# Operand blocks of the down product summed by accumulating transfers instead of VectorE, and the last pair's steps in another order

## The chip, the core and the metric

One core of a Trainium2 chip runs the whole program. The metric is the device time of one execution in microseconds. The kernel before takes 1924.49 us, the median of 3 runs (1922.67 to 1926.2).

## The reference, cut to what matters

The kernel computes one layer of a decoder for 1024 prompt tokens with 16 meta tokens ahead of them and 8 samples. Two of its parts are feed-forward blocks of the same form, one at the start and one at the end; the change touches only these.

```python
D_MODEL, D_FF = 1024, 2816

def swiglu(x, wg, wu, wd):
    return (jax.nn.silu(x @ wg) * (x @ wu)) @ wd

h = h + 0.5 * swiglu(rmsnorm(h, n1), w1g, w1u, w1d)     # first FFN, 1048 token columns here
...                                                     # HGRN2 and Mamba-2 groups, output projection
h = h + 0.5 * swiglu(rmsnorm(h, n2), w2g, w2u, w2d)     # second FFN, 1032 token columns here
```

All arithmetic is float32 in effect: each operand of a matmul is split into a high and a low part, and three matmuls (high by high, high by low, low by high) make one product.

## The kernel before, in words

**How a feed-forward block is tiled.** `ffn` takes the 22 column tiles of gate and up as 11 pairs of tiles (a and b), and then `down`. Each 2 by 2 block product is done with seven block products instead of eight, which needs sums of blocks as operands. The products of a pair are numbered 1 to 7. In `chained_pair` the string `STEPS[kind]` gives their order for the four kinds of pair, `plain`, `first`, `both` (all the middle ones) and `last`. A name such as `a5` is product 5 of tile a and makes two steps (one for each half c of the tokens), each of 12 matmuls of 262 or 258 columns; `N15` or `M4` is one step with products of the same scheme applied a second time, inside product 2 (N) or 3 (M); it has 6 matmuls for each digit. A pair of kind `both` or `first` has 28 steps.

**What sets the order.** The order is written out by hand. `Steps.run` emits, before step i, everything that was placed at i, then the matmuls of the step, then its evacuation. The tables `PLAIN`, `FIRST`, `BOTH`, `LAST` and `DOWN` place each small piece of work at a step counted from the pair's (or down's) first step; a number past the pair's end falls into the next pair. In the names of the pairs' tables, d loads a weight block, s sums two of them, h and l make the high part (ScalarE) and the low part (VectorE), g multiplies the gate by the norm and applies silu, p multiplies gate by up into the hidden tile, S and D are the stores and sums below, R is the restore below. TensorE, VectorE, ScalarE and SyncE then do their instructions in the order in which they were emitted; the order on GpSimd's queue is left to the scheduler.

**PSUM banks.** In the pairs there are two double banks for accumulation. Products 1, 6, 7 and 4 of a tile share one, 5 and 3 another. A new one can begin only when one of the two has been read for the last time.

**The hidden blocks.** A pair leaves four blocks of 128 x 524 (or 516): a0, a1, b0, b1, in two tiles of the tag "s" (8 slots, six of which hold operands of the inner products during the middle pairs). `down` reads them as the right operands of its seven products, from seven DRAM tensors in `Hidden.d`: operand 1 is a0, 2 is b0, 3 is b1, 7 is b1+a1, 5 is a1+a0, 6 is b1+a1+a0 and 4 is b0+b1+a1+a0. Before the change VectorE makes the four sums in place (`Hidden.sum_`, L1070), and SyncE stores each operand (L1073) between them. `down` (L1107) then loads each operand in six groups (L1090), and ScalarE and VectorE split them (L1094, L1098).

**Keep and restore.** The inner products M overwrite the first half of one operand of product 3. GpSimd's queue copies it to DRAM beforehand (`keep`, L580), and in the last pair, which computes product 3 again in the plain way, copies it back (`restore`, L585).

The functions that the diff touches follow, with the lines of the profile.

## Time and profile before

The profiled execution took 1926.8 us by the clock of the runs, and its span in the profile is 1925.1 us.

| | |
|---|---|
| median of 3 runs | 1924.49 us |
| profiled execution / its span | 1926.8 / 1925.1 us |
| TensorE (PE) busy | 1896.4 us, 99% |
| VectorE (DVE) busy | 1561.9 us, 81% |
| ScalarE (ACT) busy | 942.1 us, 49% |
| GpSimd (POOL) busy | 87.3 us, 5% |
| bytes moved | 260.61 MB, mean 135 GB/s |
| first FFN: pairs / down | to about 472 us / 472 to about 698 us |
| second FFN: pairs / down | about 1205 to 1681 us / 1681 us to the end |

How to read it: matmuls are pipelined, so a busy TensorE is not one at its peak. The number of matmuls in a stretch of fixed length tells more: a stretch of 5 us at full pace shows 43 or 44 of them (those that reach over an edge are counted in both stretches). "PEclk" is the share of its full clock that TensorE was granted. "A <- B" in a view of waits reads: A stood idle until B ended.

### The profile page before, as it was taken

How to read it: one execution, taken by the hardware profiler on the slowest of the kernel's cores; microseconds unless marked ns; L12 is line 12 of the kernel's file. 1: busy time of each engine (PE TensorE's matmuls, PEld its weight loads, DVE VectorE, ACT ScalarE, POOL GpSimd, SP SyncE). 2: the span in 40 equal slices, each digit the busy share in tenths (PEclk: the TensorE clock that was granted, in tenths of full speed). 3: DMA queues.
4: the chain of work that ended last, by engine and by line, in shares of the span. 5: the costliest groups of instructions: out<-in, count | busy, mean ns of one | idle time of the engine just before them, and what ended most of it. 6: DMA issues, size and time to landing. Idle time of an engine off the chain costs nothing.

```text
span 1925.1 us, 41201 instructions
## 1 busy us (share of the span) xinstructions
PE 1896.4 (99%) x16480; PEld 1861.2 (97%) x16480; DVE 1561.9 (81%) x2953; ACT 942.1 (49%) x1856; POOL 87.3 (5%) x167
## 2 busy tenths in 40 slices
PE   9999999999999999999999999999999999999998
PEld 8999999998999999999999989999999999899997
DVE  7899999998688877576776667989999999868965
ACT  7644444444533644466554465743444444453353
POOL 3000000000000410000000002200000000000000
PEclk9999999999999999999999999999999999999999
DMA  8242323346977551132444254323234233597862
GB/s 240 67 125 84 111 84 112 92 120 180 279 219 258 162 164 51 50 101 71 133 139 113 58 167 149 101 84 98 83 99 116 83 116 100 166 278 219 281 183 79
DMA packets 325801, 260.61 MB, mean 135 GB/s; under 512 B 17953, under 2 KB 299809, under 8 KB 325601
## 3 DMA queue, kind: packets, MB, share of 16 engines
q1 hardware_dynamic: 324213, 255.80, 44.2%
q8 instruction: 129, 2.11, 0.5%
q0 software_dynamic: 1376, 2.17, 0.4%
q14 instruction: 63, 0.52, 0.1%
q10 hardware_dynamic: 20, 0.01, 0.0%
HBM read 192.91 MB, written 65.08 MB: 134 GB/s over the span
## 4 chain that ended last, share of the span: by engine, by line
PE 86%; DVE 7%; DMA 3%; ACT 2%; issue 1%; SPq 0%; DVEq 0%; POOL 0%; ACTq 0%; POOLq 0%
PE acc L163 24%; PE acc L165 23%; PE acc L164 23%; PE mis L165 3%; PE mis L163 3%; PE mis L164 3%; DMA hd<-s 1%; DMA u<-hd 1%; DVE t L806 1%; PE mis L2108 1%; DVE u L1098 1%; DVE ws L470 1%; DVE r L462 1%; ACT u L348 1%; PE mis L1734 0%
## 5 line engine op out<-in xcount | busy, mean ns | idle before, releaser
L163 PE MATMUL acc<-u,ws 128*128 128x258 f32 (+4 forms) x3922 | 1150.3, 294 | 4.8 <-DVE t L806 1.9
L165 PE MATMUL acc<-u,ws 128*128 128x258 f32 (+4 forms) x3922 | 1137.6, 290 | 5.4 <-DVE ws L470 5.3
L164 PE MATMUL acc<-u,ws 128*128 128x258 f32 (+4 forms) x3922 | 1136.7, 290 | 1.9 <-DVE u L1098 1.6
L163 PEld LDWEIGHTS acc<-u,ws 128*128 128x128 f32 x3922 | 741.4, 189 | 13.0 <-issue 3.4
L164 PEld LDWEIGHTS acc<-u,ws 128*128 128x128 f32 x3922 | 744.1, 190 | 4.3 <-DVE u L1098 2.1
L165 PEld LDWEIGHTS acc<-u,ws 128*128 128x128 f32 x3922 | 740.4, 189 | 6.9 <-DVE ws L470 6.5
L466 ACT CAST ws<-r 128x512 fp32r<-128x512 f32 x232 | 143.1, 622 | 246.2 <-DVE r L462 107.0
L470 DVE TENSOR_TENSOR ws<-r,ws 128x512 fp32r<-128x512 f32 x232 | 157.7, 689 | 12.9 <-ACT ws L466 12.7
L462 DVE TENSOR_TENSOR r<-r,r 128x512 f32<-128x512 f32 x168 | 116.0, 692 | 6.2 <-DMA r<-in_w_ffn_up_dram 5.3
L1098 DVE TENSOR_TENSOR u<-u,u 128x1048 fp32r<-128x1048 f32 (+3 forms) x84 | 96.8, 1159 | 20.2 <-ACT u L1094 20.2
L819 ACT COPY t<-acc 128x524 f32<-128x524 f32 (+1 forms) x116 | 68.4, 590 | 84.8 <-PE acc L165 83.7
L873 ACT ACTIVATE t<-t 128x524 f32<-128x524 f32 (+1 forms) x80 | 51.2, 639 | 94.8 <-DVE t L806 94.6
L1094 ACT CAST u<-u 128x1048 fp32r<-128x1048 f32 (+3 forms) x84 | 82.8, 988 | 21.5 <-DMA u<-hd 21.4
L158 DVE TENSOR_TENSOR ws<-r,ws 128x512 fp32r<-128x512 f32 x88 | 61.0, 704 | 35.0 <-ACT ws L157 33.9
L165 PE MATMUL mis<-u,ws 128*128 128x258 f32 (+1 forms) x310 | 87.9, 284 | 0.5 <-DVE ws L615 0.5
L1162 ACT CAST ws<-u 128x512 fp32r<-128x512 f32 (+1 forms) x72 | 42.1, 585 | 94.7 <-DVE u L1157 91.4
L163 PE MATMUL mis<-u,ws 128*128 128x258 f32 (+1 forms) x310 | 88.0, 284 | 0.0
L164 PE MATMUL mis<-u,ws 128*128 128x258 f32 (+1 forms) x310 | 87.8, 283 | 0.0
L806 DVE TENSOR_TENSOR t<-t,u 128x524 f32<-128x524 f32 (+1 forms) x120 | 83.6, 697 | 2.0
L1191 DVE SCALAR_TENSOR_TENSOR s<-acc,s 128x524 f32<-128x524 f32 (+3 forms) x86 | 53.9, 650 | 32.0 <-PE acc L165 31.7
L1162 ACT CAST ws<-r 128x512 fp32r<-128x512 f32 (+1 forms) x84 | 48.1, 581 | 62.2 <-DVE r L1157 31.9
L1167 DVE TENSOR_TENSOR ws<-r,ws 128x512 fp32r<-128x512 f32 (+1 forms) x84 | 57.0, 694 | 19.1 <-ACT ws L1162 19.0
(486 smaller groups left out, 2734.4 us busy)
## 6 DMA issues: line engine op xcount, KB each, us to landing
r<-in_w_ffn_down_dram SPq DMA_DIRECT2D x128, 256.0 KB
hd<-s SPq DMA_DIRECT2D x93, 258.0 KB
r<-in_w_ffn_gate_dram SPq DMA_DIRECT2D x88, 256.0 KB
r<-in_w_ffn_up_dram SPq DMA_DIRECT2D x88, 256.0 KB
hd<-s SPq DMA_DIRECT2D x77, 262.0 KB
u<-hd SPq DMA_DIRECT2D x36, 516.0 KB
u<-hd SPq DMA_DIRECT2D x28, 524.0 KB
r<-in_w_in_dram SPq DMA_DIRECT2D x56, 256.0 KB
```

The costliest lines, as they stand in the source:

```text
L158: self.nc.vector.tensor_sub(lo, src, hi.bitcast(F32))
L163: mm(ps, whi, xhi, start=first, stop=False, skip_group_check=more)
L164: mm(ps, whi, xlo, start=False, stop=False, skip_group_check=more)
L165: mm(ps, wlo, xhi, start=False, stop=last, skip_group_check=more)
L462: self.K.nc.vector.tensor_tensor(self.raw[p], self.raw[x], self.raw[y], op)
L466: self.K.nc.scalar.copy(self.w[p][:, : self.n * P], self.raw[p])
L470: self.K.nc.vector.tensor_sub(t[:, 512 : 512 + w], self.raw[p], t[:, :w].bitcast(F32))
L806: nc.vector.tensor_mul(t, t if src is None else src, spread.lanes(int(n[1]), slice(0, 2)))
L819: nc.scalar.copy(temp(x, {1: "z", 6: "v", 7: "w"}[p]), ps)
L1094: K.nc.scalar.copy(hi, lo.bitcast(F32))
L1098: K.nc.vector.tensor_sub(lo, lo.bitcast(F32), hi.bitcast(F32))
L1162: nc.scalar.copy(w[p, j, g][:, : n * P], src)
```

## The change

1. The four sums leave VectorE. `Hidden.put` stores a first block into each of the seven DRAM tensors from SyncE (S1, S2, S3, S4, S5, S6, S7), and then adds the other blocks to those tensors with transfers of GpSimd's queue that accumulate in DRAM (A5, A6, A7, A4, then B6, B4, then C4). A transfer that adds to a tensor waits for the one before on the same tensor. There are 88 fewer instructions on VectorE, 154 more transfers on GpSimd's queue, and 154 stores as before.
2. In the last pair product 3 of each tile comes ahead of product 4: "a5 M4 a3 a4 b1 N15" for "a5 M4 a4 b1 a3 b6 N15", and "N4 b3 b4" at the end for "b4 N4 b3".
3. The restored half is written over another operand of M (product 5's, in a slot of the tag "s"), which is free earlier: the restore stands at step 4 and no longer at step 13. The second half (c = 1) of product 3 of tile b, and of tile a, reads its first two blocks from there.
4. All five tables place their pieces anew.

```diff
-def product(K, ps, w, op, n, first, last, more=False):
+def product(K, ps, w, op, n, first, last, more=False, k0=0):
...
     def restore(self):
-        for x, d in self.kept:
+        for x, (_, d) in zip(self.op[5], self.kept):
             self.K.nc.gpsimd.dma_start(x, d)
...
-    "last": "a1 M15 a6 M62 a7 M73 a5 M4 a4 b1 a3 b6 N15 b7 N62 b5 N73 b4 N4 b3",
+    "last": "a1 M15 a6 M62 a7 M73 a5 M4 a3 a4 b1 N15 b6 N62 b7 N73 b5 N4 b3 b4",
...
 FIRST = {
...
-    33: "ga0 Mh3 Ml2", 34: "pa0", 35: "Ml3 S1", 37: "ga1 S2", 40: "gb1", 43: "pb1", 45: "S3 pa1", 47: "D7", 49: "S7", 50: "D6 D5", 51: "D4 S5",
-    52: "S4", 55: "S6",
+    30: "S2", 31: "Mh2", 33: "ga0 Ml2", 34: "Mh3 pa0 Ml3", 37: "ga1 S1", 40: "gb1", 43: "pb1", 45: "pa1", 46: "S5", 47: "S3 S7 S6", 49: "A7 A6 A4",
+    51: "A5", 52: "B6 B4", 55: "C4",
 BOTH = {
...
-    48: "D5", 49: "S7", 50: "D6 S5", 53: "D4 S4", 59: "S6",
+    46: "A5 A7 A6", 47: "S3", 49: "B4", 50: "B6 C4",
 LAST = {
...
-    15: "Nh3 N- Nl1", 17: "hb5 Nl3", 18: "Nh2", 19: "ga1 Nl2", 20: "hb4 lb5", 22: "pa1", 23: "lb4", 26: "hb3", 27: "ga0", 28: "pa0", 30: "lb3 S1",
-    31: "gb0 pb0", 32: "gb1", 34: "S2 pb1", 36: "S3 D7", 37: "D5 S7", 39: "S5", 40: "D6", 42: "S6 D4 S4",
+    14: "N- Nh3", 15: "lb6 ga1 Nl1", 18: "Nh2 pa1 Nl2", 19: "Nl3", 20: "hb5", 22: "lb5", 24: "hb3 hb4", 25: "ga0 lb3", 27: "lb4 pa0", 28: "S5",
+    29: "gb0 S1", 31: "gb1", 32: "pb0 S2", 33: "pb1", 34: "S4", 36: "S3 S7 S6", 38: "A5 A4 A7", 39: "A6 B4", 41: "B6", 45: "C4",
...
-        product(K, ps[:, c], lefts[x].w[p], ops[c].op[p], 4, p == b, True, p != b)
+        if (kind, p, c) == ("last", 3, 1):
+            for (hi, lo), k0 in ((inners["M"].op[5], 0), ([t[:, 2 * K.Q :] for t in ops[c].op[p]], 2)):
+                w = lefts[x].w[p]
+                product(K, ps[:, c], w, (hi, lo), 2, False, k0 == 2, True, k0)
+        else:
+            product(K, ps[:, c], lefts[x].w[p], ops[c].op[p], 4, p == b, True, p != b)
...
-    def sum_(self, hid, p):
-        t, x = (self.block(hid, n) for n in {7: (3, 12), 5: (12, 1), 6: (7, 1), 4: (2, 6)}[p])
-        self.K.nc.vector.tensor_add(t, t, x)
-    def store(self, i, hid, p):
-        self.K.nc.sync.dma_start(self.d[p][:, :, i, :], halves(self.block(hid, p)))
+    def put(self, i, hid, name):
+        p, n = int(name[1]), {"S1": 0, "S5": 1, "S2": 2, "S4": 2, "S3": 3, "S7": 3, "S6": 3, "A5": 0, "A7": 1, "A6": 1, "A4": 3, "B6": 0, "B4": 1, "C4": 0}[name]
+        t = halves(hid[n // 2][0][:, n % 2 * 2 * self.K.Q : n % 2 * 2 * self.K.Q + 2 * self.K.Q])
+        if name[0] == "S":
+            self.K.nc.sync.dma_start(self.d[p][:, :, i, :], t)
+        else:
+            self.K.nc.gpsimd.dma_start(self.d[p][:, :, i, :], t, accum_op=ALU.add)
```

Three places show how the instructions move. The first is VectorE's queue in the last pair of the first FFN where tile a gives way to tile b. The line numbers shift by two to five: L824 and L834 of before are L829 and L839, L877 is L879. A row of L806 with an "acc" as source reads product 4 from its bank for the last time; L824 and L834 (now L829 and L839) do so for products 3 and 5; L462 sums two weight blocks, L470 makes a low part. Before:

```order
L834 TENSOR_TENSOR t_5448<-acc_5477,t_5448 128x524
L806 TENSOR_TENSOR t_5448<-t_5448,u_846 128x524
L470 TENSOR_TENSOR ws_5491<-r_5395,ws_5491 128x512
L637 TENSOR_TENSOR t_5257<-mis_5343,t_5257 128x262
L806 TENSOR_TENSOR t_5257<-t_5257,u_846 128x524
L462 TENSOR_TENSOR r_5264<-r_5475,r_5264 128x512
L806 TENSOR_TENSOR t_5548<-acc_5310,u_846 128x524
L877 TENSOR_TENSOR s_5413<-t_5013,t_4958 128x524
L877 TENSOR_TENSOR s_5308<-t_5257,t_5198 128x524
```

After:

```order
L462 TENSOR_TENSOR r_5293<-r_5505,r_5293 128x512
L470 TENSOR_TENSOR ws_5539<-r_5339,ws_5539 128x512
L462 TENSOR_TENSOR r_5554<-r_5425,r_5293 128x512
L829 TENSOR_TENSOR t_5419<-acc_5507,t_5419 128x524
L879 TENSOR_TENSOR s_5336<-t_5287,t_5228 128x524
L879 TENSOR_TENSOR s_5443<-t_5038,t_4981 128x524
L601 TENSOR_TENSOR r_5273<-r_5273,r_5425 128x256
L602 TENSOR_TENSOR r_5273<-r_5273,u_1545 128x256
L470 TENSOR_TENSOR ws_5551<-r_5293,ws_5551 128x512
L806 TENSOR_TENSOR t_5419<-t_5419,u_846 128x524
L615 TENSOR_TENSOR ws_5568<-u_1545,ws_5568 128x512
L806 TENSOR_TENSOR t_5621<-acc_5341,u_846 128x524
```

Before, products 5 and 3 of tile a hold their bank (acc_5477) until a3, which stands behind b1, so b1 takes the bank that product 4 leaves (L806 from acc_5310). Now a3 has left its bank (L829, acc_5507) eight rows ahead of product 4's row (L806 from acc_5341), and b1 takes that one; the whole of a4 stands between a3 and b1.

The second is VectorE's queue at the end of the same pair. Before, ws_5778 is the low part for product 3 of tile b, the pair's last product; now ws_5775 is that low part and ws_5777 is the one for product 4, which is the pair's last. L637 is a piece of an inner product, L1098 (now L1095) and L1167 (L1164) split operands and weights of `down`. Before:

```order
L834 TENSOR_TENSOR t_5714<-acc_5741,t_5714 128x524
L806 TENSOR_TENSOR t_5714<-t_5714,u_846 128x524
L637 TENSOR_TENSOR t_5337<-mis_5674,t_5337 128x262
L637 TENSOR_TENSOR t_5337<-u_1544,t_5337 128x262
L637 TENSOR_TENSOR t_5589<-u_1544,t_5589 128x262
L806 TENSOR_TENSOR t_5337<-t_5337,u_846 128x524
L1098 TENSOR_TENSOR u_5641<-u_5641,u_5640 128x1048
L877 TENSOR_TENSOR s_5697<-t_5337,t_5548 128x524
L806 TENSOR_TENSOR t_5827<-acc_5559,u_846 128x524
L1167 TENSOR_TENSOR ws_5762<-r_5661,ws_5762 128x512
L637 TENSOR_TENSOR t_5589<-mis_5666,t_5589 128x262
L470 TENSOR_TENSOR ws_5778<-r_5554,ws_5778 128x512
```

After:

```order
L806 TENSOR_TENSOR t_5369<-t_5369,u_846 128x524
L470 TENSOR_TENSOR ws_5775<-r_5554,ws_5775 128x512
L839 TENSOR_TENSOR t_5773<-acc_5805,t_5773 128x524
L806 TENSOR_TENSOR t_5773<-t_5773,u_846 128x524
L470 TENSOR_TENSOR ws_5777<-r_5483,ws_5777 128x512
L879 TENSOR_TENSOR s_5659<-t_5369,t_5621 128x524
L1095 TENSOR_TENSOR u_5703<-u_5703,u_5702 128x1048
L637 TENSOR_TENSOR t_5652<-mis_5668,t_5652 128x262
L1164 TENSOR_TENSOR ws_5803<-r_5591,ws_5803 128x512
```

The low part stood eleven instructions behind product 5's evacuation (L834) and now stands ahead of it (L839); the low part for the product that comes last now stands two behind it.

The third is GpSimd's queue from the keeping on. The names hd_109, hd_111, hd_112 and hd_114 are the operands 6, 5, 7 and 4. Before, the two copies out and the two back are followed at once by work of the groups behind the FFN:

```order
L580 DMA kp_1214<-u_546 128x524
L580 DMA kp_1215<-u_548 128x524
L585 DMA u_548<-kp_1215 128x524
L585 DMA u_546<-kp_1214 128x524
L232 TENSOR_TENSOR t_7573<-t_7573,t_7577 128x262
L232 TENSOR_TENSOR t_7575<-t_7575,t_7580 128x262
```

After, the part that belongs to the pair of kind `first`, with what each transfer waits for (DMASW is an earlier transfer of this queue, DMAHW one of SyncE's stores):

```order
L1071 DMA hd_114<-s_1876 256x1x262 [waits DMAHW6_49,DMASW7_49,DVE_49]
L1071 DMA hd_114<-s_1985 256x1x262 [waits DMASW7_49,DMASW0_49,DVE_49]
L1071 DMA hd_111<-s_1985 256x1x262 [waits DMAHW5_49]
L1071 DMA hd_114<-s_1985 256x1x262 [waits DMASW2_49,DMASW0_49]
L1071 DMA hd_112<-s_1985 256x1x262 [waits DMAHW0_49,DMASW3_49]
L1071 DMA hd_109<-s_1985 256x1x262 [waits DMAHW1_49]
L1071 DMA hd_109<-s_1985 256x1x262 [waits DMASW4_49]
```

There are now seven transfers for each pair; here they stand as A4, B4, A5, C4, A7, A6, B6, in a pair of kind `both` as A4, B4, A5, A7, A6, C4, B6. The multiplication that first writes the next pair's hidden tile (L879) waits for the transfers that read the same slot.

More of the change, by code (lines that the diff above doesn't have):

```diff
@@ L485, in plan @@
                 S.before(s0 + d, lambda p=p, fn=fn: fn(p))
-def product(K, ps, w, op, n, first, last, more=False):
+def product(K, ps, w, op, n, first, last, more=False, k0=0):
     for k in range(n):
         ks = slice(k * K.Q, k * K.Q + K.Q)
-        wh, wl = (w[:, o + k * P : o + k * P + P] for o in (0, 512))
+        wh, wl = (w[:, o + (k0 + k) * P : o + (k0 + k) * P + P] for o in (0, 512))
         K.mm3(ps, wh, wl, op[0][:, ks], op[1][:, ks], first and k == 0, last and k == n - 1, more)
@@ L863, in do @@
             return
-        if c == "S":
-            hidden.store(i, hid, int(n))
-            return
-        if c == "D":
-            hidden.sum_(hid, int(n))
+        if c in "SABC":
+            hidden.put(i, hid, name)
             return
@@ L1060, in __init__ @@
         self.d = {p: K.dram.tile([P, 2, FP, self.K.Q], F32, name=K.uid("hd")) for p in ORDER}
-    def block(self, hid, p):
-        n = {1: 0, 12: 1, 5: 1, 2: 2, 4: 2, 3: 3, 7: 3, 6: 3}[p]
-        return hid[n // 2][0][:, n % 2 * 2 * self.K.Q : n % 2 * 2 * self.K.Q + 2 * self.K.Q]
-    def sum_(self, hid, p):
-        t, x = (self.block(hid, n) for n in {7: (3, 12), 5: (12, 1), 6: (7, 1), 4: (2, 6)}[p])
-        self.K.nc.vector.tensor_add(t, t, x)
-    def store(self, i, hid, p):
-        self.K.nc.sync.dma_start(self.d[p][:, :, i, :], halves(self.block(hid, p)))
+    def put(self, i, hid, name):
[5 more added lines that the diff above has]
+            self.K.nc.gpsimd.dma_start(self.d[p][:, :, i, :], t, accum_op=ALU.add)
     def jobs(self, S, i, hid, e0, e1):
-        for p, at in ((1, e0 + 2), (3, e1 + 1), (2, e1 + 2), (7, e1 + 5), (5, e1 + 6), (6, e1 + 9), (4, e1 + 11)):
-            if p > 3:
-                S.before(at - (2 if p == 4 or p == 6 else 3), lambda p=p: self.sum_(hid, p))
-            S.before(at, lambda p=p: self.store(i, hid, p))
+        for at, names in (e0 + 2, "S1"), (e1 + 1, "S3 S7 S6"), (e1 + 2, "S2 S4 S5"), (e1 + 5, "A5 A7 A6 A4"), (e1 + 8, "B6 B4"), (e1 + 11, "C4"):
+            for name in names.split():
+                S.before(at, lambda name=name: self.put(i, hid, name))
     def load(self, place, p, at):
```

46 rows, old and new, of tables (BOTH, DOWN, FIRST, LAST) are left out of this document.

## The prediction

> **What bounds the kernel now.** I read the page first, its busy shares and its chain of waits:
>
> ```profile
> span 1925.1 us, 41201 instructions
> PE 1896.4 (99%) x16480; PEld 1861.2 (97%) x16480; DVE 1561.9 (81%) x2953; ACT 942.1 (49%) x1856; POOL 87.3 (5%) x167
> ...
> PE 86%; DVE 7%; DMA 3%; ACT 2%; issue 1%; SPq 0%; DVEq 0%; POOL 0%; ACTq 0%; POOLq 0%
> ```
>
> TensorE sets the end: it has 86% of the chain, VectorE 7%, transfers 3%. The change takes no matmul away, so it can gain only where TensorE stands idle or slow. Next come windows. A stretch of middle pairs:
>
> ```profile
> 350.00:400.00 50.00, 50.00 (x412) 49.99 (x411) 45.05 (x86) 22.17 (x45) 0.00 (x0) 1.00 0.38 113
> ```
>
> TensorE is busy throughout at full clock, so a matmul costs 50/412 = 0.121 us, and VectorE is at 90%. Nothing is left to gain there. Now the last pair of the first FFN in steps of 5 us, and behind the "..." the last rows of the same table for the second FFN (1650 to 1690 us):
>
> ```profile
> 440.00:445.00 5.00, 4.05 (x33) 3.84 (x32) 4.93 (x9) 2.23 (x4) 1.09 (x2) 1.00 0.42 110
> 445.00:450.00 5.00, 5.00 (x43) 5.00 (x42) 4.25 (x9) 0.90 (x2) 0.00 (x0) 1.00 0.68 172
> 450.00:455.00 5.00, 4.68 (x39) 4.48 (x37) 3.06 (x5) 2.26 (x4) 0.00 (x0) 1.00 0.71 255
> 455.00:460.00 5.00, 4.01 (x31) 3.81 (x32) 3.04 (x6) 1.39 (x3) 0.00 (x0) 1.00 0.71 209
> 465.00:470.00 5.00, 4.10 (x34) 3.89 (x33) 4.87 (x9) 3.33 (x6) 0.00 (x0) 1.00 0.70 174
> 470.00:475.00 5.00, 3.84 (x21) 3.85 (x22) 4.29 (x8) 0.64 (x1) 0.00 (x0) 0.72 0.72 199
> 475.00:480.00 5.00, 5.00 (x41) 5.00 (x40) 4.74 (x7) 1.46 (x3) 0.00 (x0) 0.94 0.77 240
> sum 40.00, PE 35.70 PEld 34.86 DVE 33.00 ACT 16.73 POOL 1.09; mean PE 4.46 PEld 4.36 DVE 4.12 ACT 2.09 POOL 0.14
> ...
> 1675.00:1680.00 5.00, 3.12 (x26) 2.92 (x25) 5.00 (x9) 2.62 (x4) 0.00 (x0) 1.00 0.65 191
> 1680.00:1685.00 5.00, 4.83 (x27) 4.83 (x28) 4.30 (x7) 0.64 (x1) 0.00 (x0) 0.66 0.55 142
> sum 40.00, PE 35.66 PEld 34.83 DVE 32.20 ACT 16.09 POOL 1.02; mean PE 4.46 PEld 4.35 DVE 4.02 ACT 2.01 POOL 0.13
> ```
>
> Here TensorE is idle for 40 − 35.70 = 4.3 us and 40 − 35.66 = 4.3 us. On top the granted clock drops: (1 − 0.72) x 5 + (1 − 0.94) x 5 = 1.7 us in the first, (1 − 0.66) x 5 = 1.7 us in the second. The last pairs lose 2 x 6.0 = **12.0 us** together. What ended the idle time, first for 420 to 560 us, then for 1640 to 1720 us (waited for: total, times, longest):
>
> ```profile
> PE acc L165 <- DVE ws L470: 2.1, 1, 2.1
> PE mis L163 <- ACT u L640: 1.0, 1, 1.0
> PE acc L163 <- DVE t L806: 0.9, 1, 0.9
> PE acc L163 <- ACT t L819: 0.3, 1, 0.3
> ...
> PE acc L165 <- DVE ws L470: 2.0, 1, 2.0
> PE acc L163 <- DVE t L806: 1.0, 1, 1.0
> PE mis L163 <- ACT u L640: 1.0, 1, 1.0
> PE acc L163 <- ACT t L819: 0.3, 1, 0.3
> ```
>
> Four waits, the same in both FFNs: 2.1 + 1.0 + 0.9 + 0.3 = 4.3 us, which is the idle time. The largest comes last; rows of VectorE's timeline, and the matmul that waits:
>
> ```profile
> 463.79 0.70 DVE L834 TENSOR_TENSOR t<-acc,t 128x524 f32<-128x524 f32 x1 [0.20 <-PE acc L165]
> ...
> 470.42 0.68 DVE L470 TENSOR_TENSOR ws<-r,ws 128x512 fp32r<-128x512 f32 x1
> 471.16 0.39 PE L165 MATMUL acc<-u,ws 128*128 128x262 f32 x1 [2.05 <-DVE ws L470]
> ```
>
> From b5's evacuation at 463.79 to the end of product 3's low part at 471.1, VectorE works 7.3 us without a gap, while TensorE has only N73, b4 and N4 to do, 42 matmuls or 5.1 us. It stands 2.05 us, and right behind this the clock drops.
>
> **The change, part by part.**
>
> *Order and restore in the last pair.* Each wait is taken by itself. (1) L806 is product 4's evacuation, whose bank b1 takes. After the change b1 takes the bank that a3 leaves, and a4's 24 matmuls (2.9 us) stand between; the evacuation is preceded by about three VectorE instructions of 0.7 us (2.1 us), so some 0.4 to 0.8 us are left over: 0.9 and 1.0 us gained, narrowly. (2) L470: the low part for b3 now stands ahead of b5's evacuation. The one for b4, which is last, ends three instructions behind it, 2.1 us, while b4's start comes N4 and b3 later, 30 matmuls or 3.6 us. Spare: 1.5 us. Gained: 2.1 and 2.0 us and the clock, 1.7 each. (3) L819 and L640: ScalarE copies b6's bank ahead of b7; N62 now stands between, 12 matmuls or 1.5 us, against 0.3 us of wait; and M's and N's digits have moved apart. Gained: 0.3 and, less surely, 1.0 us. The matmuls that read the restored half come nine steps behind the restore, 9 x 1.2 us or more, while a copy back lands within 6.3 us:
>
> ```profile
> L585 POOL DMA_DIRECT2D u<-kp x4: 543/544/545, 440.4 to 1650.6; - x4
> ...
> DMA to landing us min/median/max: 3.2/3.7/6.3
> ```
>
> So the restore costs nothing; if it landed at twice the longest, 12.6 us, product 3 of a would wait some 2 us in each FFN. All four waits gone give −12.0 us. The least is what (2) alone gives, 2 x (2.05 + 1.7) = 7.5 us, or none if the new places make VectorE late elsewhere. I take 85%: **−10.2 us**, as two of the four have under 1 us to spare.
>
> *The 88 sums leave VectorE.* The groups by line of the sums and of the stores:
>
> ```profile
> L1070 DVE TENSOR_TENSOR s<-s,s x44: 685/697/708, 103.4 to 1697.5; 128x524 f32<-128x524 f32 x22, 128x516 f32<-128x516 f32 x22
> L1070 DVE TENSOR_TENSOR s<-s x44: 685/696/703, 105.2 to 1699.7; 128x524 f32<-128x524 f32 x22, 128x516 f32<-128x516 f32 x22
> L1073 SPq DMA_DIRECT2D hd<-s x154: 512/519/1326, 90.5 to 1700.4; - x154
> ```
>
> 88 x 0.697 = 61 us, 4 x 0.70 = 2.8 us a pair. In the middle pairs TensorE never waits for VectorE, so they hide behind the matmuls: **0 us**. Their removal is part of the gain in the last pair, where it is counted already. The stores on SyncE's queue stay 154.
>
> *154 accumulating transfers on GpSimd's queue.* Issuing: 154 x 0.54 us (L585's row) = 84 us on an engine that is 5% busy: 0. Landing is the open cost; nothing in the trace accumulates. The nearest rows are the copies of the same size, 3.7 us median and 6.3 at most. An accumulating transfer must read its target too: from 3.7 us (the read costs nothing) to 7.4 (everything twice), and above that if the queue is busy. It counts since transfers onto one tensor go one after the other, and the multiplication that writes the slot in the next pair waits on VectorE, with everything queued behind it. In a pair of kind `first` the queue's chain is A4, B4, A6, B6 with two further issues of 0.54 us between: 4L + 1.1 us. From A4's place to that multiplication there are 205 matmuls, 24.9 us: in time up to L = 5.9. In `both` it is A4, A6, B6 with three issues, 3L + 1.6 against 215 matmuls, 26.1 us: in time up to L = 8.2. I take L = 5, between the median and the worst copy, nearest to both: **0 us**. At 7.4, allowing 2 us in which VectorE may be late without TensorE noticing (three of its instructions), `first` costs 4 x 7.4 + 1.1 − 24.9 − 2 = 3.8 us once per FFN, 7.6 in all.
>
> *Traffic at down's start.* The chain and the windows of early `down`:
>
> ```profile
> 488.73 8.06 DMA u<-hd
> ...
> 500.00:550.00 50.00, 49.15 (x401) 48.73 (x400) 39.49 (x59) 25.32 (x40) 0.00 (x0) 1.00 0.99 288
> ```
>
> The transfer engines are at 99%, and the chain passes through a load of an operand. The last pair's seven accumulations fall just ahead of it, beside seven stores as before. Their bytes, 7 x 262 KB = 1.83 MB, are additional; at 288 GB/s that is 6.4 us per FFN if TensorE waits for all of it, 12.8 in both, and 0 if they fit in ahead of 500 us, where the share is 0.7 (the rows above). A gain is excluded, for no byte is saved. I take 1 us per FFN, near the lower end, since the row shows TensorE idle for only 0.85 us in 50 even at 99%: **+2 us**.
>
> *Sum:* −10.2 + 0 + 0 + 2 = −8.2 us. The profiled execution took 1926.8 us, so 1918.6; it lies 2.3 us above the median of the runs, which makes 1924.5 − 8.2 = **1916.3 us**.
>
> **The rivals.**
>
> *Landing is slow and the pairs wait for it (slower).* Each accumulation takes L = 8 us or more. From 4L + 1.1 − 24.9 − 2 per FFN, the gain of 8.2 is eaten at L = 7.5, and the change is slower by more than 3.8 us from L = 8.0. At 8.3 it costs 7.4 x 2 = 15 us, 1931 us; at 9 `both` is late too, by 27 + 1.6 − 26.1 − 2 = 0.5 us in 14 pairs, 20.4 + 7.0 = 27 us, 1944 us. For it: chains of four, a read of the target, and 6.3 us already for one plain copy. Against it: the share of the transfer engines in the middle pairs is 0.38, so 3.7 is the copy to compare with.
>
> *Down's operands come late, the gain goes back there (no change).* −10.2 + 12.8 = +2.6, 1927 us. For it: the 99% and the chain through hd. Against it: the last pair's accumulations are issued ahead of the full stretch.
>
> *The clock does not come back with the wait (faster, less).* The drop of the clock stands behind the waits of 2.05 us in both FFNs and behind none of the waits of 1 us; I count it as that wait's own. If something else brings it, 3.4 us of the 12.0 stay: (12.0 − 3.4) x 0.85 = 7.3, less 2, −5.3 us, 1919.2 us. [...]
>
> *The new places stall VectorE in the last pair (little or nothing).* The spare 0.4 us of b1 and the ScalarE copies fall through, half of the gain stays: −5 + 2 = −3 us, 1921 us.
>
> **How the numbers follow.** The forecast 0.52, its own range 1910 to 1921 us (the gain whole with nothing lost at `down`, −12; to half of it with 2 us lost, −3); the slow landing 0.18; the late operands 0.17; the clock 0.08; the stalls 0.05. A measurement of this kernel tells 0.2%, 3.8 us, from no change, so faster is below 1920.6. Faster: 0.50 of the forecast's 0.52 and 0.07 of the clock's 0.08, 0.57. Same: the rest of these two (0.03), the late operands (0.15) and the stalls (0.04), and no landing, 0.22. Slower: the landing (0.18), the worse part of the late operands (0.02) and of the stalls (0.01), 0.21. The range goes from 1909 us (all the waits, the clock and a part of the waits early in `down`, where VectorE now has fewer instructions) to 1933 us, L = 8.5; beyond lie half of the landing and a few hundredths below.
>
> **What would show it.** In the windows of 440 to 480 us, 43 matmuls in each 5 us and a clock of 1.00; no L470 and L806 of 1 us and more among TensorE's waits; VectorE at about 83% instead of 90% in the middle pairs, with TensorE unchanged at 412 in 50 us. The transfers onto hd from GpSimd's queue with a landing under 6 us and no wait of VectorE's multiplication (L879) for them. In 500 to 550 us, at least 400 matmuls. The prediction is wrong if landing exceeds 7.5 us and multiplications of the middle pairs show idle time ended by a transfer, or if the idle time of TensorE between 480 and 560 us grows by more than 3 us.

## The result, and the profile after

The changed kernel takes 2186.82 us (median of 4 runs, 2184.56 to 2187.9), the kernel before 1924.76 us in the same comparison: a ratio of 1.136, with an interval of 1.134 to 1.138. It is **262 us slower**; forecast were 1916.3 us and a range up to 1933. The page of the changed kernel:

```profile
span 2185.0 us, 41415 instructions
...
PE 1944.7 (89%) x16480; PEld 1901.2 (87%) x16480; DVE 1506.6 (69%) x2865; ACT 942.8 (43%) x1856; POOL 257.0 (12%) x321
```

TensorE is busy for 1944.7 us, 48.3 more than before with the same 16480 matmuls, and idle for 2185.0 − 1944.7 = 240.3 us, where it was 28.7. So 212 us of the loss are waits and 48 us are matmuls at a lower clock (0.948 in the mean over the kernel, 0.997 before). It is low behind the waits: TensorE stands for 9.50 us until 287.97 us, and from 287 to 290 us the clock is 0.50, from 290 to 295 us 0.88. The same 50 us of middle pairs as in the prediction:

```profile
350.00:400.00 50.00, 41.46 (x325) 40.89 (x324) 32.86 (x64) 16.80 (x35) 7.63 (x7) 0.93 0.58 118
```

There are 325 matmuls in place of 412. The loss lies in the middle pairs, which were at full pace and of which the forecast said that nothing changes. What the engines waited for (total, times, longest):

```profile
POOL hd L1071 <- issue: 387.0, 88, 9.3
...
DVE s L879 <- DMA hd<-s: 175.6, 14, 13.8
...
PE acc L163 <- ACT s L1184: 50.9, 6, 22.7
```

Fourteen times, seven in each FFN and a pair apart, VectorE's multiplication into the hidden tile (L879) waits for a transfer onto hd, 12.5 us in the mean, and TensorE then waits for a low part that stands behind it on VectorE (L615, 121.8 us in 14 waits). Later, in `down`, the tiles that follow in the same slots wait as well (L1184). The first row is the odd one. GpSimd's queue stood idle ahead of 88 of the 154 accumulating transfers without any wait that the profile can name. The transfers themselves (one line's instructions, then the landing times):

```profile
L1071 POOL DMA_DIRECT2D hd<-s x154: 1065/1086/1166, 101.3 to 1978.7; - x154
...
DMA to landing us min/median/max: 4.1/4.5/10.1
```

A median landing of 4.5 us is even below the 5 us that I took. Now GpSimd's timeline in one pair of kind `both`, A4, B4, A5, A7, A6, C4, B6, and VectorE's multiplication in the next pair:

```profile
247.29 1.09 POOL L1071 DMA_DIRECT2D hd<-s  x1 [16.56 <-DVE s L879]
254.49 1.08 POOL L1071 DMA_DIRECT2D hd<-s  x1 [6.11 <-DMA hd<-s]
261.20 1.09 POOL L1071 DMA_DIRECT2D hd<-s  x1 [5.62 <-issue]
266.35 1.08 POOL L1071 DMA_DIRECT2D hd<-s  x1 [4.06 <-issue]
272.50 1.09 POOL L1071 DMA_DIRECT2D hd<-s  x1 [5.07 <-issue]
276.98 1.08 POOL L1071 DMA_DIRECT2D hd<-s  x1 [3.39 <-issue]
281.58 1.09 POOL L1071 DMA_DIRECT2D hd<-s  x1 [3.51 <-issue]
...
286.08 0.70 DVE L879 TENSOR_TENSOR s<-t,t 128x524 f32<-128x524 f32 x1 [13.35 <-DMA hd<-s]
```

A5, A7 and A6 go to three tensors, and the profile names no other transfer that they wait for; yet each starts 5.2 to 6.7 us behind the one ahead. The seven take 34.3 us from the first start to the last, and 4.5 us later the multiplication begins. It follows the one of the pair before (234.21) by 51.9 us, where a pair took 39.4. The question for the experiments: why does GpSimd's queue send one accumulating transfer at a time?

### The profile page after: what moved, and what is told of

It reads as the page before. It is cut to its first block, busy times and chain, and to the rows that moved or that the text cites. A ratio compares the mean times of both kernels' runs of the same rounds, so it can differ in the third digit from the quotient of the medians.

```text
span 2185.0 us, 41415 instructions
## 1 busy us (share of the span) xinstructions
PE 1944.7 (89%) x16480; PEld 1901.2 (87%) x16480; DVE 1506.6 (69%) x2865; ACT 942.8 (43%) x1856; POOL 257.0 (12%) x321
## 3 DMA queue, kind: packets, MB, share of 16 engines
HBM read 192.91 MB, written 106.08 MB: 137 GB/s over the span
## 5 line engine op out<-in xcount | busy, mean ns | idle before, releaser
L163 PE MATMUL acc<-u,ws 128*128 128x258 f32 (+4 forms) x3914 | 1164.2, 298 | 71.1 <-ACT s L1184 50.9
L164 PE MATMUL acc<-u,ws 128*128 128x258 f32 (+4 forms) x3914 | 1148.4, 294 | 5.3 <-DVE u L1095 5.0
L165 PE MATMUL acc<-u,ws 128*128 128x258 f32 (+4 forms) x3914 | 1147.3, 293 | 5.1 <-DVE ws L470 5.0
L163 PEld LDWEIGHTS acc<-u,ws 128*128 128x128 f32 x3914 | 755.1, 193 | 84.1 <-ACT s L1184 52.1
L164 PEld LDWEIGHTS acc<-u,ws 128*128 128x128 f32 x3914 | 757.4, 194 | 8.4 <-DVE u L1095 6.4
L165 PEld LDWEIGHTS acc<-u,ws 128*128 128x128 f32 x3914 | 752.8, 192 | 5.8 <-DVE ws L470 5.4
L1071 POOL DMA_DIRECT2D hd<-s x154 | 167.3, 1086 | 1020.0 <-issue 387.0
L165 PE MATMUL mis<-u,ws 128*128 128x258 f32 (+1 forms) x310 | 94.9, 306 | 122.2 <-DVE ws L615 121.8
L879 DVE TENSOR_TENSOR s<-t,t 128x524 f32<-128x524 f32 (+1 forms) x80 | 54.4, 695 | 177.3 <-DMA hd<-s 175.6
L470 DVE TENSOR_TENSOR ws<-r,ws 128x512 fp32r<-128x512 f32 x232 | 158.9, 688 | 25.7 <-ACT ws L466 25.7
L165 PEld LDWEIGHTS mis<-u,ws 128*128 128x128 f32 x310 | 62.5, 202 | 125.8 <-DVE ws L615 125.7
L462 DVE TENSOR_TENSOR r<-r,r 128x512 f32<-128x512 f32 x168 | 115.8, 690 | 27.4 <-DMA r<-in_w_ffn_up_dram 27.1
L1095 DVE TENSOR_TENSOR u<-u,u 128x1048 fp32r<-128x1048 f32 (+3 forms) x84 | 97.1, 1157 | 30.1 <-ACT u L1091 29.9
L824 ACT COPY t<-acc 128x524 f32<-128x524 f32 (+1 forms) x116 | 68.3, 589 | 86.8 <-PE acc L165 85.7
L163 PE MATMUL mis<-u,ws 128*128 128x258 f32 (+1 forms) x310 | 90.9, 293 | 14.7 <-ACT u L640 14.5
L232 POOL TENSOR_TENSOR t<-t,t 128x262 f32<-128x262 f32 (+1 forms) x56 | 54.7, 986 | 317.6 <-ACT t L231 314.3
L164 PE MATMUL mis<-u,ws 128*128 128x258 f32 (+1 forms) x310 | 90.2, 291 | 0.0
L1164 DVE TENSOR_TENSOR ws<-u,ws 128x512 fp32r<-128x512 f32 (+1 forms) x72 | 46.2, 648 | 62.8 <-ACT ws L1159 62.8
```

Source lines behind the costliest of these rows:

```text
L163: mm(ps, whi, xhi, start=first, stop=False, skip_group_check=more)
L164: mm(ps, whi, xlo, start=False, stop=False, skip_group_check=more)
L165: mm(ps, wlo, xhi, start=False, stop=last, skip_group_check=more)
L232: K.nc.gpsimd.tensor_add(self.sq[q], self.sq[q], t)
L462: self.K.nc.vector.tensor_tensor(self.raw[p], self.raw[x], self.raw[y], op)
L470: self.K.nc.vector.tensor_sub(t[:, 512 : 512 + w], self.raw[p], t[:, :w].bitcast(F32))
```

## The experiments

### What the transfers cost, and what the rest of the change is worth

The first kernel, `probe`, prices the transfers by themselves:

```diff
 (kernel before)
+    def probe(self, i, hid):        # pairs 3 to 9, when operand 1 is stored; T, U: scratch tensors
+        for j in range(6):
+            i == 3: dma(T[j], halves(a0))                       i == 4: the same with accum_op=ALU.add
+            i == 5: dma(U[j], a0)                               i == 6: the same with accum_op=ALU.add
+            i == 7: dma(U[j][:, :Q], a0[:, :Q], accum_op=ALU.add)
+            i == 8: dma(U[j][:32], a0[:32], accum_op=ALU.add)
+            i == 9: dma(T[j], halves(a0)), every second one with accum_op=ALU.add
```

> The kernel before, with six GpSimd transfers added in each middle pair of both FFNs, to tensors that nothing reads, no two of a pair onto the same one; their source is the pair's block a0. One form a pair, in this order: plain 256 rows of 262, accumulating 256 rows of 262, plain 128 rows of 524, accumulating 128 x 524, accumulating 128 x 262, accumulating 32 x 524, then plain and accumulating 256 x 262 in turn. Theory Q (each accumulating transfer holds GpSimd's queue until the one ahead of it has landed, whatever tensor it goes to): starts of accumulating ones 4.5 us or more apart although they are independent, plain ones 0.6 us (128 rows) and 1.1 us (256 rows) apart. Theory R (256 rows are too many for the queue, accumulating or not): plain and accumulating of 256 rows both 4 us or more apart, 128 rows about 1 us or less. Theory C (only a chain onto one tensor waits): all starts 1.1 us apart or less. The time stays within 15 us of before under each, for only the next pair's first multiplication into a0 can be held up.

Measured: 1946.8 us in one run, beside 1925.4 for the kernel before, 21 us more where at most 15 were expected. The extra time comes mostly from the last form, which stood ahead of the restore on the queue (TensorE waits 6.6 and 6.7 us for its copies in the two last pairs); the starts are what counts. GpSimd's timeline, the pairs 3 to 7 in order (an "xN" row is N instructions back to back):

```profile
195.46 2.14 POOL L1069 DMA_DIRECT2D pt<-s  x3 [153.76 <-DVE s L877]
199.53 0.68 POOL L1069 DMA_DIRECT2D pt<-s  x1 [1.94 <-issue]
...
235.63 1.14 POOL L1071 DMA_DIRECT2D pt<-s  x1 [32.34 <-DVE s L877]
241.14 1.12 POOL L1071 DMA_DIRECT2D pt<-s  x1 [4.37 <-issue]
...
276.86 3.27 POOL L1073 DMA_DIRECT2D pu<-s  x6 [14.14 <-DVE s L877]
316.13 2.63 POOL L1075 DMA_DIRECT2D pu<-s  x3 [36.00 <-DVE s L877]
323.04 0.87 POOL L1075 DMA_DIRECT2D pu<-s  x1 [4.28 <-issue]
...
356.60 2.61 POOL L1077 DMA_DIRECT2D pu<-s  x3 [30.09 <-DVE s L877]
361.63 2.62 POOL L1077 DMA_DIRECT2D pu<-s  x3 [2.42 <-issue]
```

None of the three theories holds as it stood. Accumulating transfers with 256 rows start one by one, 5.5 us apart in the rows shown, although the targets differ (against theory C). With 128 rows three go back to back, then comes a gap of 4.3 us (against Q: it isn't the adding as such). With half the bytes in the same 128 rows it is again three and a gap, of 2.42 us, so the bytes don't decide how many go together. With 32 rows all six go, 4.78 us in all. Plain transfers of 256 rows also go three and then wait, 1.94 us (against R in its simple form), and six plain ones of 128 rows go without a gap. One account fits all of these, theory B, which is my reading of the starts (no view shows the places themselves): the queue has room for a limited number of rows in flight, and an accumulating row takes two places. One accumulating transfer of 256 rows (512 places) fits, two (1024) don't; three of 128 (768) fit, four (1024) don't; three plain ones of 256 (768) fit, four (1024) don't. So read, the limit is between 768 and 1023 places.

The second kernel, `nosums`, leaves the accumulating transfers out:

```diff
 (changed kernel)
-        else:
-            self.K.nc.gpsimd.dma_start(self.d[p][:, :, i, :], t, accum_op=ALU.add)
```

> The changed kernel without its 154 accumulating transfers; the first stores stay, so operands 4 to 7 of down are single blocks and not sums. If the transfers alone make the change slow, this shows what the rest does: 1914 to 1917 us by the prediction's own terms (-10.2 us in the last pairs, nothing at down). If the new tables or the restore are at fault as well, it stays above 1930 us.

Measured: 1926.36 us, a ratio of 1.0005 (0.9996 to 1.0015): no change. So the 154 transfers cost 2186.8 − 1926.4 = 260 us, all of the loss, and the rest of the change gains nothing, where 8 to 10 us were forecast. Windows of the last pair in both FFNs, of the start of `down` and of middle pairs:

```profile
350.00:400.00 50.00, 50.00 (x413) 50.00 (x412) 42.74 (x83) 22.65 (x45) 0.00 (x0) 1.00 0.38 107
440.00:480.00 40.00, 39.13 (x317) 38.92 (x318) 31.26 (x52) 17.52 (x30) 0.00 (x0) 1.00 0.65 194
480.00:500.00 20.00, 17.48 (x125) 16.74 (x124) 10.55 (x14) 13.31 (x21) 0.00 (x0) 0.91 0.91 266
1650.00:1690.00 40.00, 37.47 (x309) 36.96 (x308) 32.64 (x55) 17.87 (x31) 0.00 (x0) 1.00 0.56 165
```

In the last pair the gain is there: the kernel before had 274 and 278 matmuls in the two windows of 40 us, now there are 317 and 309, (43 + 31) x 0.121 = 9.0 us. Of the four waits that the prediction names there none is left, and the clock is 1.00. Most of this gain is lost again. At the start of `down` the kernel before did 162 matmuls in the same 20 us:

```profile
480.00:500.00 20.00, 19.70 (x162) 19.49 (x161) 9.57 (x13) 10.08 (x17) 0.00 (x0) 1.00 0.87 263
```

Now there are 125, 37 x 0.121 = 4.5 us less: TensorE waits 1.76 us for an operand that ScalarE splits late (L1089), and ScalarE itself waited for its load from hd. In the second FFN it is 144 instead of 165 (1690 to 1710 us), 2.5 us. A third piece is lost elsewhere, in the first pairs of the second FFN, where 20 us (1290 to 1310) hold 137 matmuls instead of 165, 3.4 us. There a weight block of up lands late, and TensorE stands until its low part is made:

```profile
1297.19 0.39 PE L165 MATMUL acc<-u,ws 128*128 128x258 f32 x1 [2.05 <-DVE ws L470]
```

And one wait is new in the last pair itself:

```profile
439.65 0.70 DVE L839 TENSOR_TENSOR t<-acc,t 128x524 f32<-128x524 f32 x1
...
440.40 0.39 PE L163 MATMUL acc<-u,ws 128*128 128x262 f32 x1 [1.10 <-DVE t L839]
```

That matmul is the first of a3. Products 5 and 3 share a bank, and "a5 M4 a3" leaves only the 6 matmuls of M4 between them, so a3 waits until product 5 has been read. At the end of tile b, "b5 N4 b3", it is the same, 0.46 us in the first FFN and 1.25 in the second.

The third kernel, `plain`, makes the transfers plain ones:

```diff
 (changed kernel)
-            self.K.nc.gpsimd.dma_start(self.d[p][:, :, i, :], t, accum_op=ALU.add)
+            self.K.nc.gpsimd.dma_start(self.d[p][:, :, i, :], t)
```

> The changed kernel with the same 154 transfers on GpSimd's queue, with the same waits and sizes, but plain ones that overwrite instead of adding (so operands 4 to 7 of down hold the last block written and not the sum). Theory Q (only accumulating ones hold the queue): the three landings of the chain, at 3.7 us each, fit into a pair, and the time is 1914 to 1925 us. Theory R (rows or GpSimd's queue as such): 2150 us or more, as the changed kernel.

Measured: 1955.6 us, 1.014 (1.011 to 1.016). Neither 1914 to 1925 nor 2150: 231 of the 260 us are gone. By B a plain row takes half the places, and three transfers fit instead of one, as in `probe`. It fits B, not Q, by which the plain ones would have been free.

The fourth, `lastonly`, was meant to show the gain of the last pair alone:

```diff
 (kernel before, with the new "last" order, restore, product 3 and LAST table; the sums stay on VectorE)
-    27: "lb4 pa0", 28: "S5", 29: "gb0 S1", ... 32: "pb0 S2", 33: "pb1", 34: "S4", 36: "S3 S7 S6", 38: "A5 A4 A7", 39: "A6 B4", 41: "B6", 45: "C4",
+    27: "lb4 pa0", 28: "S1", 29: "gb0", ... 32: "pb0", 33: "pb1 S2", 35: "S3 D7", 36: "D5 S7", 38: "S5", 39: "D6", 41: "S6 D4 S4",
```

> The kernel before with the second and third part of the change only: the last pair's order 3 ahead of 4, the restored half over product 5's operand, and the changed table of the last pair with the sums left on VectorE at the end of it. By the prediction's term: 10.2 us faster, 1914.6 us, with TensorE's idle time between 440 and 480 us falling from 4.3 us to about 1 us. If VectorE's four sums in that pair are what makes it late, half of that, about 1919 us.

Measured: 1944.5 us, 1.009 (1.008 to 1.011): slower, a miss. VectorE's timeline at the start of `down` shows the largest part, and it is my placing of the sums:

```profile
486.97 0.70 DVE L1075 TENSOR_TENSOR s<-s,s 128x524 f32<-128x524 f32 x1 [7.59 <-DMA hd<-s]
487.59 0.69 DVE L1172 TENSOR_TENSOR ws<-r,ws 128x512 fp32r<-128x512 f32 x1
```

A sum in place (L1075) waits 7.6 us until the store of the old contents has landed, and the low part that TensorE needs (L1172) stands right behind it; TensorE waits 7.3 us there. The run can't show what the order of the products is worth.

### The number of rows, and the number of transfers

If B holds, fewer rows a block must give most of the time back. `rows128` changes the layout of the seven tensors, so that both halves of a block's row lie side by side:

```diff
 (changed kernel)
-        self.d = {p: K.dram.tile([P, 2, FP, self.K.Q], F32, name=K.uid("hd")) for p in ORDER}
+        self.d = {p: K.dram.tile([P, FP, 2, self.K.Q], F32, name=K.uid("hd")) for p in ORDER}
 (put)
-            self.K.nc.gpsimd.dma_start(self.d[p][:, :, i, :], t, accum_op=ALU.add)
+            self.K.nc.gpsimd.dma_start(self.d[p][:, i].rearrange("p c t -> p (c t)"), t, accum_op=ALU.add)
 (load)
-            K.nc.sync.dma_start(op[c][g][1].bitcast(F32), self.d[p][:, c, i : i + n].rearrange("p n t -> p (n t)"))
+            K.nc.sync.dma_start(op[c][g][1].bitcast(F32).rearrange("p (n t) -> p n t", n=n), self.d[p][:, i : i + n, c])
```

> The changed kernel with the seven DRAM tensors laid out so that a block is 128 rows of 524 and not 256 of 262 (the loads of down then read rows of 262 with a stride); the same 154 accumulating transfers, bytes and waits. Theory B, formed from the probe (the queue takes new transfers only while the rows in flight stay under a limit, an accumulating row counting for two: one transfer of 256 rows or three of 128 at a time): up to three in flight, A4 to B6 in about 17 us, the pairs no longer wait, and the time is that without the sums, 1926 us, plus up to 20 us at down's start: 1926 to 1946 us. If it is the adding itself that holds the queue: 2150 us or more, as in the changed kernel.

Measured: 1947.0 us, 1.012 (1.010 to 1.013): 240 of the 262 us come back, with the same adding, the same bytes and the same chains. B's range was 1926 to 1946, so this is 1 us above it.

`nosums128` is the same without the accumulating transfers.

> The same layout of 128 rows without the 154 accumulating transfers (operands 4 to 7 of down are single blocks). If the layout does not matter to the loads: 1926 us, as the kernel without the transfers and the old layout; if strided rows make down's loads slower, up to 20 us more. Its difference to the run before it is what the accumulating transfers cost by themselves once three of them can be in flight.

Measured: 1915.8 us, 0.995 (0.994 to 0.997). Here the last pairs' gain lasts. The time is close to the forecast's 1916.3 us, but for a kernel that does no sums at all and in a layout that the forecast did not have, so the agreement is luck and confirms no term. The transfers cost 31 us even when three fit.

`fouracc` keeps four of the seven transfers of a pair.

```diff
 (changed kernel)
-        else:
+        elif name[0] == "A":
             self.K.nc.gpsimd.dma_start(self.d[p][:, :, i, :], t, accum_op=ALU.add)
```

> The changed kernel with four of the seven transfers a pair (A5, A7, A6, A4; B and C are left out, so the operands of down lack blocks), 256 rows each. Theory B: 4 x 5 us after a start 13 us behind the pair's first multiplication end at 33 + 4.5 us, just inside the 39.3 us of a pair, so the middle pairs go at full pace: 1926 to 1950 us. If each of the 154 transfers cost its share alike, 1926 + 260 x 4/7 = 2075 us.

Measured: 1953.0 us, 1.015 (1.013 to 1.017), just above the range of B and far from 2075. The cost doesn't go by the count: four transfers a pair cost 27 us over `nosums`, seven cost 260. By B four one by one fit into a pair and seven don't.

### The room of the queue itself

Both versions build the program with `dynamic_dma_scratch_size=1024`. `ring2048` doubles this number, `ringrows128` does so in the kernel with 128 rows:

```diff
 (changed kernel, and the kernel with 128 rows)
-    nc = _bacc.Bacc("TRN2", target_bir_lowering=False, num_devices=1, dynamic_dma_scratch_size=1024)
+    nc = _bacc.Bacc("TRN2", target_bir_lowering=False, num_devices=1, dynamic_dma_scratch_size=2048)
```

> The changed kernel with one number changed: the room that the program sets aside for GpSimd's transfers (dynamic_dma_scratch_size) is 2048 and not 1024; rows, waits and bytes as changed. Theory B with this room as its limit: about twice the rows in flight, so three accumulating transfers of 256 rows instead of one (as three of 128 rows in the run with the other layout): the middle pairs no longer wait, and the time comes down to that of the plain transfers with their own gaps or of the 128 rows, 1940 to 1965 us. If the queue's limit is something else (only the number of rows, whatever the room): 2187 us, as changed.

> The changed kernel with both: 128 rows a block and room 2048, so all seven of a pair's transfers fit at once. With 128 rows and room 1024 it is 1947 us, 31 us above the same kernel without the transfers. If the rest of the loss is still the queue's room: near 1916 to 1930 us. If it is the chains (a transfer onto a tensor waits until the one before it has landed) or the traffic: 1940 to 1950 us, little changed.

Measured: `ring2048` 1968.3 us, 1.021 (1.019 to 1.024), `ringrows128` 1948.9 us, 1.012 (1.011 to 1.014). This one number takes 218 us off the changed kernel. GpSimd's timeline of `ring2048` in a pair of kind `both` shows three accumulating transfers of 256 rows back to back, where there was one:

```profile
256.61 1.06 POOL L1071 DMA_DIRECT2D hd<-s  x1 [19.21 <-DVE s L879]
264.45 3.28 POOL L1071 DMA_DIRECT2D hd<-s  x3 [6.78 <-DMA hd<-s]
271.07 1.07 POOL L1071 DMA_DIRECT2D hd<-s  x1 [3.34 <-issue]
```

Behind the three the next waits 3.34 us. Counted as in B, the limit with 2048 lies between 1536 places (three of 512) and 2047; with 1024 it was 768 to 1023. Both fit a limit just under the number itself; that is a reading of two points. That the number sets the queue's room is my reading as well; what the runs show is that doubling it let three of these transfers start together instead of one and moved the time by 218 us.

With 128 rows the doubled number changes nothing (1948.9 against 1947.0 us), so the 31 us that stay over `nosums128` don't come from it. What they are shows in the waits of `ringrows128`:

```profile
POOL hd L1072 <- DMA hd<-s: 269.7, 55, 30.0
...
DVE r L462 <- DMA r<-in_w_ffn_up_dram: 17.6, 11, 5.3
```

and of `nosums128`:

```profile
DVE r L462 <- DMA r<-in_w_ffn_up_dram: 3.3, 4, 1.8
```

GpSimd hardly waits without a named cause any more (5.9 us, 387.0 in the changed kernel), and the multiplications wait for the chains for 0.7 us in all. Instead the weights come late: VectorE waits 17.6 us for weights of up, against 3.3. Windows of the first pairs and of the last one with the start of `down`, for `ringrows128`,

```profile
110.00:130.00 20.00, 19.37 (x156) 18.87 (x155) 15.62 (x27) 6.59 (x12) 5.21 (x6) 1.00 0.97 226
...
450.00:500.00 50.00, 43.90 (x329) 42.75 (x329) 28.28 (x44) 22.22 (x37) 9.55 (x11) 0.93 1.06 277
```

have a share of the transfer engines of 0.97 and 1.06 where matmuls are lost; in a middle pair (300 to 350 us) it is 0.66 and the pace is full. In `nosums128` the first row's share is 0.35 and the last's 0.87. The ends of an FFN are not the only place. In a middle pair of the second FFN a block of up lands late as well, and VectorE waits 5.3 us for it and TensorE stands for 4.05 us. While the load is under way, from 1400 to 1410 us, the share of the transfer engines is 1.09 and 1.01:

```profile
1415.08 0.55 PE L163 MATMUL acc<-u,ws 128*128 128x258 f32 x1 [4.05 <-DVE t L839]
```

SyncE, whose queue issues the weights, is not what holds them: it waits 405.8 us in all for L879 ahead of stores in `ringrows128` and 392.7 us in `nosums128`, and none of its longer waits names a transfer onto hd. So the likely cause of the 31 us is traffic: the accumulating transfers crowd out the weights, mostly at both ends of an FFN. No run took the traffic away while leaving the transfers, so this part is read from the waits and not shown by itself.

### The wait in the last pair, moved alone

`lb3early` moves one piece of the kernel before:

```diff
 (kernel before, LAST)
-    26: "hb3", 27: "ga0", 28: "pa0", 30: "lb3 S1",
+    26: "hb3", 27: "lb3 ga0", 28: "pa0", 30: "S1",
```

> The kernel before with one piece moved: the low part for product 3 of tile b in the last pair stands at step 27 and not at step 30, six instructions earlier on VectorE. The prediction's price of that wait: 2.05 us and 1.7 us of clock in each FFN, 2 x 3.75 = 7.5 us, so 1918 us. If the clock drops for another reason, 4.1 us, 1921 us. If VectorE's work that it passes is needed as soon, the wait moves and the time stays at 1925 us.

Measured: 1926.5 us, 1.0006 (0.9997 to 1.0015): no change. Windows and TensorE's waits (420 to 560 us):

```profile
465.00:470.00 5.00, 5.00 (x44) 5.00 (x43) 4.87 (x9) 2.88 (x6) 0.00 (x0) 1.00 0.68 178
470.00:475.00 5.00, 5.00 (x42) 4.80 (x41) 4.29 (x8) 1.02 (x2) 0.00 (x0) 1.00 0.74 188
475.00:480.00 5.00, 3.22 (x25) 3.00 (x26) 4.67 (x7) 1.46 (x3) 0.00 (x0) 1.00 0.80 257
```

```profile
PE acc L165 <- DVE ws L1167: 1.8, 1, 1.8
```

The 2.05 us and the low clock behind them are gone, 44 and 42 matmuls in place of 34 and 21, and 5 us later TensorE waits 1.8 us for a low part of `down`'s weights (L1167) that stands further back on the same queue. The 31 matmuls gained are lost again by 500 us: 25 in place of 41 from 475 to 480 us, 149 in place of 162 from 480 to 500. What was late was not one piece but VectorE's whole queue from 463.79 on. In the second FFN the wait moves in the same way, and there the clock falls behind it:

```profile
1690.47 0.40 PE L165 MATMUL acc<-u,ws 128*128 128x258 f32 x1 [1.80 <-DVE ws L1167]
...
1690.00:1695.00 5.00, 4.53 (x25) 4.53 (x26) 1.06 (x3) 1.50 (x3) 0.00 (x0) 0.66 0.92 298
```

### Versions that might be faster

`before128` is the kernel before with the layout of 128 rows and nothing else; `before128lb3` adds the moved piece.

```diff
 (kernel before)
-        self.K.nc.sync.dma_start(self.d[p][:, :, i, :], halves(self.block(hid, p)))
+        self.K.nc.sync.dma_start(self.d[p][:, i].rearrange("p c t -> p (c t)"), self.block(hid, p))
 (the tensors and the loads as in rows128)
```

> The kernel before with nothing changed but the layout of the seven DRAM tensors: a block is 128 rows of 524 and not 256 of 262. The kernel without the accumulating transfers gained 10.5 us from this layout (1926.4 to 1915.8 us). If that gain belongs to the stores and loads, which both have in common: about 1915 us. If it was owed to the changed tables, or to VectorE having no sums to make: 1925 us.

> The same layout with the low part of the last product placed at step 27. With the old layout that piece moved the wait of 2.05 us behind the pair, to a low part of down's weights (1.8 us), and gained nothing. If down's first weights come earlier with the new layout, up to 7 us less than the run before it; if VectorE's queue is what is late there, the same time.

Measured: 1922.65 us, 0.9989 (0.9980 to 0.9998), and 1922.96 us, 0.9994 (0.9986 to 1.0003). Of the 10.5 us that the layout gave without the transfers, some 2 are left with the old order and the sums on VectorE; the moved piece again gives nothing. One row of `before128` bears on the clock: in the first FFN the wait of 2.05 us is still there, and this time the clock stays at 1.00, with 43 matmuls from 470 to 475 us:

```profile
469.39 0.39 PE L165 MATMUL acc<-u,ws 128*128 128x262 f32 x1 [2.05 <-DVE ws L470]
```

`sums128` puts together what is left of value: the layout, the new order of the last pair with its restore, the changed tables of the last pair and of `down`, and VectorE's sums further behind the stores than in `lastonly`:

```diff
 (lastonly, with the layout of rows128 and the changed DOWN table)
-    33: "pb1 S2", 35: "S3 D7", 36: "D5 S7", 38: "S5", 39: "D6", 41: "S6 D4 S4",
+    33: "pb1 S2", 34: "S3", 39: "D7 D5", 40: "S7 S5", 45: "D6", 46: "S6 D4", 47: "S4",
```

> The changed order of the last pair, the changed tables of the last pair and of down, the restored half over product 5's operand, the layout of 128 rows, and the sums left on VectorE (in the last pair five steps behind the stores that they wait for); the other pairs' tables as before. Without any sums, with all changed tables and this layout the time was 1915.8 us; with the sums, the old order and this layout 1922.7 us. If the gain of the order survives VectorE's four sums in the last pair: about 1916 us. If it was owed to VectorE having no sums there: 1922 us or more.

Measured: 1920.98 us, 0.9977 (0.9967 to 0.9986), the fastest complete kernel here, 3.8 us ahead of the one before. Its interval overlaps that of `before128`, so how much of it is owed to the order stays open. So does what the remaining 5.2 us over `nosums128` are, which has no sums and other tables in all pairs. TensorE's waits in it (420 to 560 us):

```profile
PE acc L164 <- DVE u L1103: 2.1, 2, 1.5
PE acc L163 <- DVE t L839: 0.9, 1, 0.9
```

The wait for b4's or b3's low part and the one for L640 are gone; what stays is a3's wait for the bank and a wait in `down`.

## Why the prediction was wrong

**The step that failed** is the one on the 154 accumulating transfers on GpSimd's queue, taken at 0 us and measured at 260: it had transfers to different tensors go out back to back, and the queue took one at a time. Its parts one by one. The issue of a transfer, taken at 0.54 us from the copies (L585), is 1.09 us for 256 rows; harmless. The landing, taken at 5 us, is 4.5; right. What reading the target costs was my estimate, from nothing to 3.7 us more, and no view shows it by itself (the page counts 192.91 MB read from HBM in both kernels); beside the copies' 3.7 us the landing is 0.8 us longer. Wrong was the chain: "A4, A6, B6 with three issues, 3L + 1.6" lets A5, A7, A6 and C4 start as soon as their own waits allow. Instead the seven start one at a time, 4.5 to 7.2 us apart: 34.3 + 4.5 us in the rows above, where 3 x 4.5 + 1.6 gives 15.1. The place where it is paid is the one that the prediction names, the next pair's multiplication with its 26.1 us: a pair now takes 51.9 us and not 39.4, so 14 pairs lose some 170 of the 260 us there; the rest is lost in the other pairs and at `down`. The prediction had no row for how many transfers the queue holds at once and no term for it. The copies from which it took the issue have 128 plain rows each, by B 256 places for two, so they could not show the limit.

**The rivals.** "Landing is slow" named the right wait and the right side, but with a condition (L of 8 us or more) that the run does not meet, and a price of 15 to 27 us. It was a rival on the length of one transfer (4.5 us); the cause is how few start together (one of 256 rows). "Down's operands come late" has a part in the 31 us by which `rows128` lies over `nosums128`, and which the doubled number does not take away (`ringrows128`, 1948.9 us); I took +2 and at most 12.8. I counted the bytes of the last pair only, and the weights of the first pairs come late as well. I also took the share of the transfer engines ahead of 500 us as 0.7 from rows that end at 480; from 480 to 500 us it is 0.87 in the kernel before (the row above), so there was less room for the seven transfers than I wrote.

**The last pair, −10.2 us.** Right in place, and near in size within the pair: 9.0 us by the count of matmuls in `nosums`. It did not reach the end in `nosums` (1926.4 us): some 7 us went at the start of `down` and 3.4 in the first pairs of the second FFN. In `nosums128` (1915.8) the second of these is gone (165 matmuls from 1290 to 1310 us) and the first is smaller (145 and 162 matmuls in the two windows of 20 us). Why the layout does this no run shows. Two points of its working failed. The bank: I saw that b1 takes the one that a3 leaves, and overlooked that a3 writes the one that a5 has just filled; 0.5 to 1.3 us each time. And for what would be late next on VectorE's queue the working has a spare time for b4's low part only; `lb3early` shows the wait moving to `down`'s weights at 1.8 us.

**The sums taken off VectorE, 0 us:** right for the middle pairs. In `nosums` VectorE is busy for 42.74 of 50 us instead of 45.05 and TensorE does 413 matmuls in place of 412. The relief is 2.3 us in 50, 85% busy, where I wrote 83%.

**The clock.** The prediction counted 1.7 us of low clock as the own price of each wait of 2.05 us; the rival had the drop stay when the wait goes. Neither holds as it stands. In `lb3early` that wait is gone in both FFNs. Behind the wait of 1.8 us that takes its place in the first FFN the clock stays at 1.00; behind the one of 1.80 us in the second it falls to 0.66. In `before128` it stays at 1.00 behind a wait of 2.05 us in the first FFN. In `nosums` it falls (0.91 in the window of 480 to 500 us) behind two waits of 1.76 and 0.62 us within one microsecond. So in these runs the length of a wait from 1.8 to 2.05 us does not decide by itself whether the clock falls; what else does stays open. In the changed kernel, with waits of up to 10 us, the clock of the middle pairs is 0.93 in the window of 350 to 400 us, and TensorE is busy for 48 us more over the kernel.

## What to carry to other kernels

Ahead of moving work to a queue, ask for three numbers: how long one transfer takes, how long the chain is, and how many the queue takes at once; the last has no row in a profile in which the queue is nearly unused, and a small kernel with independent transfers of several shapes prices it in one run. A queue's idle time with no named cause ("issue", 387.0 us ahead of 88 of the 154 transfers) was here the sign that transfers were held up; fewer and longer rows gave back 240 us and the doubled number 218. And a wait on an engine that is back to back was here the first of a line: taking away the one of 2.05 us moved it to the next piece, at 1.8 us (`lb3early`).

## What was not expected of the hardware

GpSimd's queue lets few transfers go together: with 1024 one accumulating transfer of 256 rows, three of 128 and three plain ones of 256 (`probe`), with 2048 three accumulating ones of 256 (`ring2048`). I read this as rows in flight, between 768 and 1023 places and between 1536 and 2047, a plain row taking one place and an accumulating row two. In `probe` it depends neither on the bytes (128 accumulating rows of 262 and of 524 both go three at a time) nor on the target (starts 5.5 us apart onto different tensors). And blocks of 128 long rows instead of 256 short ones gave 10.5 us where nothing else had changed (`nosums` and `nosums128`), 1.7 us in the kernel before. A wait of TensorE as short as 1.80 us was followed by a clock of 0.66 over 5 us in one place, and one of 2.05 us by a full clock in another.
